# The partition sum of each conditioning gate: four paced pieces of 512 columns in place of one of 2048

## The chip, the cores and the metric

The kernel runs on one core of one Trainium2 chip. The metric is the device time of one execution in microseconds (us); less is better. The engines are TensorE (PE, its weight loads PEld), VectorE (DVE), ScalarE (ACT), GpSimd (POOL) and SyncE (SP), which run side by side and wait for each other by semaphores.

## The reference

A two-layer diffusion backbone over 256 latent and 256 context positions of width 2048. Layer 0 mixes by neighbourhood attention, layer 1 by a gated MLP (gMLP); a SwiGLU feed-forward network (FFN) follows each.

```
sh1, sc1, g1, sh2, sc2, g2 = split(silu(c) @ ada_w[i] + ada_b[i], 6)   # per layer i
y = mixer_i(h * (1 + sc1) + sh1)
h = layer_norm(ALPHA * h + g1 * y)
h = layer_norm(ALPHA * h + g2 * swiglu(h * (1 + sc2) + sh2))
...
# gMLP mixer: u, v = split(gelu(a @ w_in));  v = layer_norm(v)
#             return (u * (W_s @ v + b_s)) @ w_out          # W_s 128x128 per group
```

The change touches g1 and g2, two vectors of 2048 numbers in each layer, four "gates" in all. Each is a matrix-vector product with a matrix of 2048x2048.

## The kernel before

**Stages.** Attention comes first (up to about 590 us), then layer 0's FFN (up to some 1310), the gMLP (up to some 1690) and layer 1's FFN. In each, PE multiplies activations by a stream of weights, in pieces of 1024 columns (512 for a part of w_k). SP issues the weights' DMAs. ACT rounds each piece to a high part (L93, names beginning with h: hwq, hwf, hwgo), and DVE subtracts that from it to get the low part (L94, names beginning with l: lwk, lwq, lwf, lwgo). PE makes three matmuls for each tile: L88 high x high, L89 and L90 with one low part (which of the two is the low one depends on the stage). Activations are split by the same lines (kl, vl, tl, glgo, gld); ql is at L460.

**The conditioning work** is spread over this stream as tasks. A gate is made on DVE: the 2048 rows of its matrix come as 16 row blocks of 128 (k = 0 to 15), each in two halves of 1024 columns (ag, DMAs issued on ACT's queue at L77, four buffers, `ADA`). Each half is multiplied by a number per partition and added to `gate`, a tile of 128 partitions x 2048 columns (L176). `gate` begins at zero in all partitions but one, which holds the bias (L170, L171, on POOL). When all 32 halves are in, a sum over the 128 partitions is left; POOL makes it with one partition_all_reduce in place (L191). The result is read only in the residual at the stage's end (L569). The other four vectors of a layer are made by dot products on DVE (ad, L152).

**What sets the order.** Tasks stand in a list. `pace` divides their total weight by a number of ticks (126 for attention, 245, 62 and 170 for the stages after it); each `tick` adds that rate to a credit, and each task is put into the program when the credit holds its weight of 0.5. `need` empties the list as far as a stage requires. The DMAs of the first three tasks in the list (`FETCH`) are issued ahead. The compiler's scheduler then sets each engine's own order from the program's, by its model of what is ready; weight streams keep theirs.

Three places are spoken of in the prediction. In attention, per head, PE makes kps (keys, from ah, al and hwk, lwk), qps (queries), the scores s (from kh, kl, qh, ql), and transposes (pt, L519) of p, the softmax's numerator, which ACT makes (L509) from s and from its row maxima nm, which DVE makes (L502, L504). In the gMLP, for each block nb, PE makes sp (L858, from vv and ws), DVE makes u in place from sp and u (L859), and PE transposes u (uvt, L863) for the product with w_gout (pogo, from hwgo, lwgo, ghgo, glgo). Last, the FFN's first product pf takes hwf and lwf.

Of the kernel before, what the change touches and what calls it, by code (L numbers as in the profile page):

```python
# [23 lines left out]
NB = D // 512  # L24
# [27 lines left out]
def hybrid_kernel(ctx: ExitStack, tc: tile.TileContext, i, out):  # L52
# [20 lines left out]
    gate = {}  # L73
# [19 lines left out]
        S.copy(hi, src)  # L93
        V.tensor_tensor(lo, src, hi.bitcast(F32), ALU.subtract)  # L94

# [1 line left out]
    queue, ready = [], []  # L97
    pos = {"n": 0, "bufs": 3, "wide": None}

# [36 lines left out]
        del ready[:k]  # L136
        return got

# [1 line left out]
    loaded = {}  # L140

    def dot_task(layer, t, nt, half):
        key = (layer, t, nt, half)

        def fetch():
            src = i["ada_t"][dot_index(layer, t, nt)]
            loaded[key] = load(src[:, half * 1024 : (half + 1) * 1024], f"ad{layer}{t}{nt}{half}")

        def run():
            r = loaded.pop(key)  # L150
            o = (cols2 if half else cols)[:, layer, t, :]
            V.scalar_tensor_tensor(  # L152
                r, r, 1.0, c_bc[:, half * 1024 : (half + 1) * 1024], ALU.mult, ALU.mult,
                accum_out=o[:, nt : nt + 1],
            )
            if nt == KT - 1 and half:
                o = cols[:, layer, t, :]
                V.tensor_tensor(o, o, cols2[:, layer, t, :], ALU.add)
                V.tensor_tensor(o, o, badj[:, layer, t, :], ALU.add)
        return [(layer, t), 0.5, run, fetch]  # L160

    def gate_task(layer, t, kt, half):
        key = (layer, t, kt, half)
        sl = slice(half * 1024, (half + 1) * 1024)

        def fetch():
            if kt == 0 and half == 0:
                g = outer.tile([P, D], F32, tag="gate", name=f"gate{layer}{t}")
                gate[(layer, t)] = g
                nc.gpsimd.memset(g, 0.0)  # L170
                nc.gpsimd.dma_start(g[0:1, :], i["ada_b_row"][layer, t : t + 1, :])  # L171
            loaded[key] = load(i["ada_g"][gate_index(layer, t, kt)][:, sl], f"ag{layer}{t}{kt}{half}")

        def run():
            g = gate[(layer, t)][:, sl]
            V.scalar_tensor_tensor(g, loaded.pop(key), c_col[:, kt, 0:1], g, ALU.mult, ALU.add)  # L176
        return [(layer, t), 0.5, run, fetch]
# [7 lines left out]
        split_into(gh, gl, src)  # L185
        return gh, gl

    def sum_task(layer, t):
        def run():
            g = gate[(layer, t)]  # L190
            nc.gpsimd.partition_all_reduce(g, g, P, ReduceOp.add)  # L191
        return [(layer, t), 0.5, run, None]

    tasks, side = [], []
# [8 lines left out]
    def add_tasks(layer, *ts):  # L203
        for t in ts:
            if t in (G1, G2):
                tasks.extend(gate_task(layer, t, k, e) for k in range(KT) for e in range(2))
                tasks.append(sum_task(layer, t))
            else:
                tasks.extend(dot_task(layer, t, k, e) for k in range(KT) for e in range(2))

# [21 lines left out]
    def pace(units):  # L232
        state["rate"] = sum(t[1] for t in tasks) / units

# [1 line left out]
    for kt in range(KT):  # L236
        enqueue(i["w_kv0"][kt], f"kv{kt}", (W0,))
        for at, h, k0 in EARLY:
# [33 lines left out]
    enqueue_out(i["w_gout"], KT, "wgo")  # L272
    enqueue_ffn(1)

# [1 line left out]
    oT = outer.tile([P, NH, NT], F32, tag="xT", name="oT")  # L276
    with tc.tile_pool(name="attnX", bufs=1) as px, ExitStack() as late:
        ah = px.tile([P, KT, 512], F32R, tag="ah", name="ah")
# [153 lines left out]
        def t_tile(name):  # L432
            return mp.tile([P, 512], F32, tag="t", name=name, bufs=2)

        add_tasks(0, G1, SH2, SC2)
        add_tasks(1, SH1)
        pace(126)
        pend = []
# [363 lines left out]

            project_out(FT, lambda f: gT(f)[:, 0, :], key, name, finish, extra, last)

    # layer 0
    m = Modulated(0, 0, SH2, SC2, "f0")
    free = ExitStack()
    pw = free.enter_context(tc.tile_pool(name="pw", bufs=1))
# [3 lines left out]
    )  # L812
    affine_tasks(h_t, i["ln_row"][0], "a0")
    add_tasks(0, G2)
    add_tasks(1, SC1, SH2, SC2)
    pace(245)
# [7 lines left out]

    ffn(0, m, (0, G2), "d0", begin, free)

    # layer 1
    m = m2[0]
    affine_tasks(h_t, i["ln_row"][1], "a1")
    add_tasks(1, G1)  # L830
# [184 lines left out]
```

## Time and profile before

| | us |
|---|---|
| time, median of 3 runs | 2494.54 |
| lowest, highest | 2493.43, 2497.09 |
| profiled execution, span | 2495.6 |
| PE busy | 2422.3 |
| DVE busy | 1758.7 |
| ACT busy | 1097.2 |
| POOL busy | 110.6 |

The page of the profile gives for the profiled execution its span alone. Busy times of engines overlap, so they don't add up to the span. In the rows further below, the times in a row are the start (us from the span's begin) and how long it took; what stands in brackets is the engine's idle time just before and what ended it.

### The profile page before, as it was taken

Reading aid. Unit: us, or ns where it says so; the run is one execution under the profiler, and the core shown is the slowest. Engines: PE = TensorE matmul, PEld = TensorE weight load, DVE = VectorE, ACT = ScalarE, POOL = GpSimd, SP = SyncE. Lnnn points to the kernel's source line nnn. Section 1 sums busy time; section 2 is a strip of 40 time slices with the busy share of each in tenths; the row PEclk is TensorE's granted clock in tenths of the full one; section 3 lists DMA queues with packets and bytes.
Section 4 is the critical chain, followed back from the end, with each engine's and each line's share of the span. In section 5 each row is a group of like instructions: output and inputs, shape, how many; then the busy total and the mean of one; then the engine's idle time right before and its main releaser. Section 6 shows DMA issues by size and latency. Waiting matters only on the chain.

```text
span 2495.6 us, 38599 instructions
## 1 busy us (share of the span) xinstructions
PE 2422.3 (97%) x15254; PEld 2157.9 (86%) x15254; DVE 1758.7 (70%) x2159; ACT 1097.2 (44%) x1494; POOL 110.6 (4%) x56
## 2 busy tenths in 40 slices
PE   6999899999999999999999999899999999999998
PEld 5787788888789999999788778777899999998886
DVE  3878877777886676666778788687755555566666
ACT  3344433345553333333455554446533333344453
POOL 0000200000010020000000020020100000020000
PEclk8999999999999999999999999999999999999999
DMA  8977787777568878888888767765666666655563
GB/s 319 350 264 257 242 282 261 273 260 252 186 232 286 271 270 292 284 283 282 285 281 279 257 214 263 249 212 173 216 228 219 218 217 226 220 194 187 176 208 130
DMA packets 167422, 611.03 MB, mean 245 GB/s; under 512 B 18916, under 2 KB 21284, under 8 KB 162884
## 3 DMA queue, kind: packets, MB, share of 16 engines
q1 hardware_dynamic: 120888, 440.64, 52.8%
q10 hardware_dynamic: 46224, 167.89, 19.4%
q8 instruction: 119, 1.95, 0.3%
q14 instruction: 63, 0.52, 0.1%
q0 software_dynamic: 128, 0.03, 0.0%
HBM read 606.40 MB, written 2.10 MB: 244 GB/s over the span
## 4 chain that ended last, share of the span: by engine, by line
PE 85%; DVE 6%; DMA 5%; issue 1%; ACT 1%; POOL 0%; DVEq 0%; ACTq 0%
PE pf L90 12%; PE pf L88 12%; PE pf L89 12%; PE pod L90 6%; PE pod L89 6%; PE pod L88 6%; DMA ad<-in_ada_t 4%; PE vps L88 2%; PE vps L89 2%; PE vps L90 2%; PE gv L90 1%; PE gv L88 1%; PE gv L89 1%; PE powo L88 1%; PE kps L88 1%
## 5 line engine op out<-in xcount | busy, mean ns | idle before, releaser
L93 ACT CAST hwf<-rwf 128x1024 fp32r<-128x1024 f32 x320 | 335.8, 1049 | 556.9 <-PE pf L89 489.6
L94 DVE TENSOR_TENSOR lwf<-rwf,hwf 128x1024 fp32r<-128x1024 f32 x320 | 406.8, 1278 | 216.1 <-ACT hwf L93 215.3
L90 PE MATMUL pf<-f1h,lwf 128*128 128x256 f32 x1280 | 361.2, 282 | 0.3 <-DVE lwf L94 0.3
L90 PE MATMUL pf<-f0h,lwf 128*128 128x256 f32 x1280 | 361.1, 282 | 0.0
L88 PE MATMUL pf<-f1h,hwf 128*128 128x256 f32 x1280 | 361.0, 282 | 0.0
L88 PE MATMUL pf<-f0h,hwf 128*128 128x256 f32 x1280 | 361.0, 282 | 0.0
L89 PE MATMUL pf<-f0l,hwf 128*128 128x256 f32 x1280 | 360.7, 282 | 0.0
L89 PE MATMUL pf<-f1l,hwf 128*128 128x256 f32 x1280 | 360.6, 282 | 0.0
L152 DVE SCALAR_TENSOR_TENSOR ad<-ad,c_bc 128x1024 f32<-128x1024 f32 x192 | 233.9, 1222 | 167.6 <-DMA ad<-in_ada_t 167.3
L88 PE MATMUL pod<-hwd,ghd 128*128 128x512 f32 x684 | 267.9, 392 | 2.0 <-DVE gTb L796 2.0
L90 PE MATMUL pod<-hwd,gld 128*128 128x512 f32 x684 | 267.7, 392 | 0.4 <-DVE gld L94 0.4
L89 PE MATMUL pod<-lwd,ghd 128*128 128x512 f32 x684 | 267.8, 391 | 0.0
L94 DVE TENSOR_TENSOR lwd<-rwd,hwd 128x1024 fp32r<-128x1024 f32 x172 | 211.9, 1233 | 50.0 <-ACT hwd L93 49.2
L90 PEld LDWEIGHTS pf<-f1h,lwf 128*128 128x128 f32 x1280 | 242.5, 189 | 0.5 <-DVE lwf L94 0.5
L88 PEld LDWEIGHTS pf<-f1h,hwf 128*128 128x128 f32 x1280 | 242.6, 190 | 0.1
L89 PEld LDWEIGHTS pf<-f0l,hwf 128*128 128x128 f32 x1280 | 242.6, 190 | 0.0
L89 PEld LDWEIGHTS pf<-f1l,hwf 128*128 128x128 f32 x1280 | 242.6, 190 | 0.0
L88 PEld LDWEIGHTS pf<-f0h,hwf 128*128 128x128 f32 x1280 | 242.6, 190 | 0.0
L90 PEld LDWEIGHTS pf<-f0h,lwf 128*128 128x128 f32 x1280 | 242.6, 190 | 0.0
L176 DVE SCALAR_TENSOR_TENSOR gate<-ag,c_col,gate 128x1024 f32<-128x1024 f32 x128 | 165.1, 1296 | 87.0 <-DMA ag<-in_ada_g 86.5
L93 ACT CAST hwd<-rwd 128x1024 fp32r<-128x1024 f32 x172 | 180.0, 1046 | 43.3 <-DMA rwd<-in_w_out 19.1
L88 PEld LDWEIGHTS pod<-hwd,ghd 128*128 128x128 f32 x684 | 128.4, 188 | 30.8 <-DVE gTb L796 2.4
(331 smaller groups left out, 4568.1 us busy)
## 6 DMA issues: line engine op xcount, KB each, us to landing
rwf<-in_w_in_f SPq DMA_DIRECT2D x320, 512.0 KB
ad<-in_ada_t ACTq DMA_DIRECT2D x192, 512.0 KB
rwd<-in_w_out SPq DMA_DIRECT2D x176, 512.0 KB
ag<-in_ada_g ACTq DMA_DIRECT2D x128, 512.0 KB
rwg<-in_w_gin SPq DMA_DIRECT2D x64, 512.0 KB
ap<-in_ada_p SPq DMA_DIRECT2D x19, 1024.0 KB
rwq<-in_w_q SPq DMA_DIRECT2D x32, 512.0 KB
rwo<-in_w_o SPq DMA_DIRECT2D x32, 512.0 KB
```

The costliest lines, as they stand in the source:

```text
L88: keep(T.matmul(ps, sh, mh, start=first, stop=False))
L89: keep(T.matmul(ps, sh, ml, start=False, stop=False))
L90: keep(T.matmul(ps, sl, mh, start=False, stop=last))
L93: S.copy(hi, src)
L94: V.tensor_tensor(lo, src, hi.bitcast(F32), ALU.subtract)
L152: V.scalar_tensor_tensor(r, r, 1.0, c_bc[:, half * 1024 : (half + 1) * 1024], ALU.mult, ALU.mult, accum_out=o[:, nt : nt + 1],)
L176: V.scalar_tensor_tensor(g, loaded.pop(key), c_col[:, kt, 0:1], g, ALU.mult, ALU.add)
```

## The change

`sum_task` gets a number n and sums 512 columns of the gate; `add_tasks` puts four of them (NB is 4) behind the gate's 32 accumulations, each with a weight of 0.5 of its own. The other lines of the diff remove comments.

```
-    def sum_task(layer, t):
+    def sum_task(layer, t, n):
         def run():
-            g = gate[(layer, t)]
+            g = gate[(layer, t)][:, n * 512 : (n + 1) * 512]
             nc.gpsimd.partition_all_reduce(g, g, P, ReduceOp.add)
         return [(layer, t), 0.5, run, None]
...
                 tasks.extend(gate_task(layer, t, k, e) for k in range(KT) for e in range(2))
-                tasks.append(sum_task(layer, t))
+                tasks.extend(sum_task(layer, t, n) for n in range(NB))
```

The tasks of the attention stage weigh 66 in place of 64.5, those of the stage that ends with layer 0's FFN the same, those of the gMLP stage 18 in place of 16.5, and those of the last stage the same. As the program's order moves, so do the scheduled orders of the engines. Names carry a number at their end, which differs between the two programs.

DVE at the first gate, before (a gate row is the accumulation of one half):

```order
L94 TENSOR_TENSOR lwq_1024_2312<-rwq_1024_2309,hwq_1024_2311 128x1024
L286 TENSOR_TENSOR oT<-kps_2308,oT 128x512
L176 SCALAR_TENSOR_TENSOR gate_1471<-ag_2328,c_col,gate_1471 128x1024
L94 TENSOR_TENSOR kl_2335<-oT,kh_2334 128x512
L94 TENSOR_TENSOR lwk_0_2342<-rwk_0_2339,hwk_0_2341 128x512
L176 SCALAR_TENSOR_TENSOR gate_1471<-ag_2331,c_col,gate_1471 128x1024
L94 TENSOR_TENSOR lwq_0_2375<-rwq_0_2372,hwq_0_2374 128x1024
L460 SCALAR_TENSOR_TENSOR ql_2403<-qps_2338,qh_2402 128x256
L176 SCALAR_TENSOR_TENSOR gate_1471<-ag_2370,c_col,gate_1471 128x1024
L94 TENSOR_TENSOR lwq_1024_2411<-rwq_1024_2408,hwq_1024_2410 128x1024
L502 TENSOR_TENSOR s_2434<-s_2434,bias_2432 128x256
```

And after, at the same place:

```order
L176 SCALAR_TENSOR_TENSOR gate_1471<-ag_2331,c_col,gate_1471 128x1024
L94 TENSOR_TENSOR kl_2338<-oT,kh_2337 128x512
L94 TENSOR_TENSOR lwk_0_2345<-rwk_0_2342,hwk_0_2344 128x512
L94 TENSOR_TENSOR lwq_0_2376<-rwq_0_2373,hwq_0_2375 128x1024
L176 SCALAR_TENSOR_TENSOR gate_1471<-ag_2334,c_col,gate_1471 128x1024
L94 TENSOR_TENSOR lwq_1024_2412<-rwq_1024_2409,hwq_1024_2411 128x1024
L460 SCALAR_TENSOR_TENSOR ql_2404<-qps_2341,qh_2403 128x256
L94 TENSOR_TENSOR vl_2550<-v_2306,vh_2549 128x512
L286 TENSOR_TENSOR oT<-kps_2408,oT 128x512
L502 TENSOR_TENSOR s_2431<-s_2431,bias_2429 128x256
L502 TENSOR_TENSOR s_2443<-s_2443,bias_2429 128x256
L504 TENSOR_REDUCE nm_2436<-s_2431 128x1
```

The last accumulation of half 0 (of ag_2331 in both) moved from behind lwk to ahead of kl; that of half 1 (ag_2370 before, ag_2334 after) stays between the two lwq; ql moved behind both lwq, and vl and oT ahead of the scores.

DVE in the gMLP, at the u of the last two blocks, before:

```order
L94 TENSOR_TENSOR lwgo_1_1024_15343<-rwgo_1_1024_15340,hwgo_1_1024_15342 128x1024
L859 SCALAR_TENSOR_TENSOR u_15175<-sp_15362,bs,u_15175 128x2x128
L859 SCALAR_TENSOR_TENSOR u_15175<-sp_15373,bs,u_15175 128x2x128
L94 TENSOR_TENSOR lwgo_2_0_15396<-rwgo_2_0_15393,hwgo_2_0_15395 128x1024
L859 SCALAR_TENSOR_TENSOR u_15175<-sp_15362,bs,u_15175 128x2x128
L859 SCALAR_TENSOR_TENSOR u_15175<-sp_15373,bs,u_15175 128x2x128
L176 SCALAR_TENSOR_TENSOR gate_14025<-ag_15482,c_col,gate_14025 128x1024
L176 SCALAR_TENSOR_TENSOR gate_14025<-ag_15507,c_col,gate_14025 128x1024
L859 SCALAR_TENSOR_TENSOR u_15358<-sp_15416,bs,u_15358 128x2x128
```

And after:

```order
L94 TENSOR_TENSOR lwgo_1_1024_15355<-rwgo_1_1024_15352,hwgo_1_1024_15354 128x1024
L176 SCALAR_TENSOR_TENSOR gate_14031<-ag_15350,c_col,gate_14031 128x1024
L859 SCALAR_TENSOR_TENSOR u_15187<-sp_15377,bs,u_15187 128x2x128
L859 SCALAR_TENSOR_TENSOR u_15187<-sp_15388,bs,u_15187 128x2x128
L176 SCALAR_TENSOR_TENSOR gate_14031<-ag_15371,c_col,gate_14031 128x1024
L859 SCALAR_TENSOR_TENSOR u_15187<-sp_15377,bs,u_15187 128x2x128
L859 SCALAR_TENSOR_TENSOR u_15187<-sp_15388,bs,u_15187 128x2x128
L94 TENSOR_TENSOR lwgo_2_0_15411<-rwgo_2_0_15408,hwgo_2_0_15410 128x1024
L94 TENSOR_TENSOR glgo_4_15526<-uT,ghgo_4_15525 128x256
L859 SCALAR_TENSOR_TENSOR u_15373<-sp_15431,bs,u_15373 128x2x128
```

After, the two gate rows are the last of their halves (k = 15), and no accumulation of this gate follows; before, the two gate rows stand behind the four u, and one more accumulation, the last, follows behind the last u (not shown).

## Rows read from the trace of the kernel before

**Rows 1.** The page's busy times: engine, busy us, share of the span, instructions.

```profile
PE 2422.3 (97%) x15254; PEld 2157.9 (86%) x15254; DVE 1758.7 (70%) x2159; ACT 1097.2 (44%) x1494; POOL 110.6 (4%) x56
```

**Rows 2.** PE's waits over the whole span: what waited, its releaser, us in total, times, the longest.

```profile
PE pt L519 <- ACT p L509: 10.6, 6, 6.8
...
PE sp L858 <- DVE u L859: 5.7, 2, 4.9
...
PE kps L90 <- DVE lwk L94: 2.1, 3, 1.2
...
PE pogo L90 <- DVE glgo L94: 1.0, 1, 1.0
...
PE pf L90 <- DVE lwf L94: 0.3, 1, 0.3
```

**Rows 3.** POOL's timeline, the four sums.

```profile
267.92 12.78 POOL L191 PARTITION_ALL_REDUCE gate<-gate  x1 [110.16 <-DVE gate L176]
...
874.37 12.78 POOL L191 PARTITION_ALL_REDUCE gate<-gate  x1 [146.73 <-DVE gate L176]
...
1649.11 12.78 POOL L191 PARTITION_ALL_REDUCE gate<-gate  x1 [88.58 <-DVE gate L176]
...
2196.57 11.88 POOL L191 PARTITION_ALL_REDUCE gate<-gate  x1 [414.06 <-DVE gate L176]
```

**Rows 4.** DVE's timeline from 262 to 290 us, around the first sum.

```profile
261.46 1.28 DVE L176 SCALAR_TENSOR_TENSOR gate<-ag,c_col,gate 128x1024 f32<-128x1024 f32 x1 [1.32 <-DMA ag<-in_ada_g]
262.67 0.69 DVE L94 TENSOR_TENSOR kl<-oT,kh 128x512 fp32r<-128x512 f32 x1
263.27 0.68 DVE L94 TENSOR_TENSOR lwk<-rwk,hwk 128x512 fp32r<-128x512 f32 x1
...
265.06 1.22 DVE L94 TENSOR_TENSOR lwq<-rwq,hwq 128x1024 fp32r<-128x1024 f32 x1
...
270.73 0.68 DVE L286 TENSOR_TENSOR oT<-kps,oT 128x512 f32<-128x512 f32 x1
271.32 7.15 DVE L94 TENSOR_TENSOR lwk<-rwk,hwk 128x512 fp32r<-128x512 f32 x1
278.40 1.21 DVE L152 SCALAR_TENSOR_TENSOR ad<-ad,c_bc 128x1024 f32<-128x1024 f32 x1
```

**Rows 5.** PE's timeline in the same stretch, three of its matmuls.

```profile
264.27 0.39 PE L90 MATMUL kps<-ah,lwk 128*128 128x512 f32 x1
...
267.01 0.39 PE L90 MATMUL s<-kh,ql 128*128 128x512 f32 x1
...
280.50 0.48 PE L519 MATMUL pt<-ident,p 128*128 128x128 f32 x1 [6.80 <-ACT p L509]
```

**Rows 6.** DVE's timeline, the operation beside each of the three later sums.

```profile
875.33 10.15 DVE L94 TENSOR_TENSOR lwf<-rwf,hwf 128x1024 fp32r<-128x1024 f32 x1
...
1650.06 9.35 DVE L94 TENSOR_TENSOR glgo<-uT,ghgo 128x256 fp32r<-128x256 f32 x1
...
2197.00 9.78 DVE L94 TENSOR_TENSOR lwf<-rwf,hwf 128x1024 fp32r<-128x1024 f32 x1
```

**Rows 7.** The instructions of line 604 (counts; shortest, median and longest in ns; first and last start; form), which run beside POOL's broadcasts of 512 columns; POOL's last two broadcasts, of 2048 columns; and two DVE rows there, the first just ahead of the broadcasts and the second beside one.

```profile
L604 DVE TENSOR_TENSOR h_t<-h_t,lra x24: 677/683/1150, 708.1 to 1783.2; 128x512 f32<-128x512 f32 x24
...
2244.84 5.40 POOL L82 PARTITION_BROADCAST last_rows<-last_rows  x2 [36.39 <-DMA last_rows<-in_ln_row]
...
2244.13 0.43 DVE L94 TENSOR_TENSOR gld<-gTa,ghd 128x256 fp32r<-128x256 f32 x1
...
2248.00 2.38 DVE L94 TENSOR_TENSOR gld<-gTa,ghd 128x256 fp32r<-128x256 f32 x1
```

**Rows 8.** Windows: stretch, its length, then busy us of PE, PEld, DVE, ACT and POOL with instructions in brackets, PE's granted clock (1.00 is full), the DMA share and GB/s.

```profile
280.50:284.00 3.50, 3.50 (x13) 3.12 (x14) 3.50 (x7) 2.94 (x6) 0.20 (x1) 0.50 0.20 78
284.00:288.00 4.00, 4.00 (x22) 3.50 (x22) 3.06 (x4) 1.33 (x3) 0.00 (x0) 0.89 0.77 209
...
200.00:206.00 6.00, 3.91 (x25) 3.17 (x24) 5.56 (x8) 2.60 (x4) 0.00 (x0) 1.00 0.89 298
```

**Rows 9.** The gMLP from 1570 to 1585 us: two DMA issues on ACT's queue, and DVE up to the first u.

```profile
1571.02 0.33 ACTq L77 DMA_DIRECT2D ag<-in_ada_g  x1
...
1573.52 0.34 ACTq L77 DMA_DIRECT2D ag<-in_ada_g  x1
...
1578.12 1.28 DVE L176 SCALAR_TENSOR_TENSOR gate<-ag,c_col,gate 128x1024 f32<-128x1024 f32 x1 [3.13 <-DMA ag<-in_ada_g]
...
1580.46 0.87 DVE L859 SCALAR_TENSOR_TENSOR u<-sp,bs,u 128x256 f32<-128x256 f32 x2
```

**Rows 10.** The gMLP from 1632 to 1648 us: DVE at an accumulation, at the first two u after it, at the last u and at the last accumulation, and PE at the one wait there.

```profile
1632.16 1.28 DVE L176 SCALAR_TENSOR_TENSOR gate<-ag,c_col,gate 128x1024 f32<-128x1024 f32 x1 [2.09 <-DMA ag<-in_ada_g]
...
1634.49 0.87 DVE L859 SCALAR_TENSOR_TENSOR u<-sp,bs,u 128x256 f32<-128x256 f32 x2
...
1645.03 0.48 DVE L859 SCALAR_TENSOR_TENSOR u<-sp,bs,u 128x256 f32<-128x256 f32 x1
...
1647.72 1.28 DVE L176 SCALAR_TENSOR_TENSOR gate<-ag,c_col,gate 128x1024 f32<-128x1024 f32 x1
...
1635.03 0.48 PE L858 MATMUL sp<-vv,ws 128*128 128x256 f32 x1 [0.86 <-DVE u L859]
```

## The prediction

> **What bounds the kernel now.** I read the page's busy times first: PE is busy for 2422.3 us of a span of 2495.6, POOL, which makes the sums, for 4% [rows 1]. So the kernel is bound by TensorE, and an edit on POOL can only be worth PE's idle time, some 70 us in all, or cause more of it. Second, PE's waits by releaser [rows 2]: five lines can be tied to the places where a sum runs. Third, POOL's own timeline [rows 3]: the four sums take 12.78, 12.78, 12.78 and 11.88 us. Fourth, VectorE's rows just behind each sum's start, since nobody waits for a sum itself for hundreds of us, but VectorE stands still beside it. At the first sum, lwk<-rwk,hwk took 7.15 us where the same form took 0.68 eight us earlier [rows 4]. PE then waited 6.80 us for p at 280.50 [rows 5]. At the other three, lwf took 10.15 us, glgo 9.35 and lwf 9.78 [rows 6]; with a free port a 128x1024 subtraction takes 1.22 [rows 4] and a 128x256 one 0.43 [rows 7]. So a sum of 2048 columns holds a VectorE operation with two SBUF inputs for 10.15 - 1.22 = 8.93 us. An operation that reads PSUM is not held: oT<-kps,oT took 0.68 at 270.73, inside the sum that began at 267.92 [rows 3, 4].
>
> What the hold costs PE differs by place, by how far VectorE is ahead. First gate: 6.80 us [rows 5], and behind it a lower clock: 0.50 granted in 280.5 to 284 and 0.89 in 284 to 288 (0.50 is 1.2 GHz, 1.00 is 2.4), which loses 3.5 x 0.50 + 4 x 0.11 = 2.2 us [rows 8]. Second gate: no line of PE's waits stands there, so VectorE's lead was above 8.93. Third: 0.98 us (pogo<-glgo). Fourth: 0.3 us (pf<-lwf), a lead of about 8.56 - 0.3 = 8.3 [rows 2, 6]. All that the four sums cost is thus 6.8 + 2.2 + 1.0 + 0.3 = 10.3 us, and the change can't win more than that from them.
>
> **The change, part by part.** *Price of one piece.* No sum of 512 columns is in the trace. The bounds are 8.93 us (all of it fixed) and 8.93 / 4 = 2.23 (all of it columns). The nearest rows are POOL's broadcasts: the longest h_t subtraction beside a 512-column broadcast took 1.150 against 0.683, 0.47 more [rows 7]; gld beside one of 2048 columns (two last_rows broadcasts, 5.40 us each by the record's pair) took 2.38 against 0.43, 1.95 more [rows 7]. That is 4.2 to 1, with no fixed part to be seen. I take 2.23.
>
> *Pieces 0 and 1 start earlier.* Columns 0 to 1023 are complete with the half-0 accumulation of k = 15; only half 1 follows. So two pieces may run before the last accumulation, two after.
>
> *First gate.* I step through VectorE's order of after with the durations of before. Half 0 ends at 262.75 (its wait was for its DMA, which the change hardly moves) [rows 4]. Piece 0 holds from about 263.35 (kl runs first) to 265.6; lwk (0.68) is done at 266.2, where PE's L90 of kps stood at 264.27: 1.9 lost [rows 5]. lwq runs (1.22); piece 1 holds 267.4 to 269.6 with the half-1 accumulation behind it, done 270.9; lwq, then ql at 272.4, which the order has moved behind them. PE's L90 of s, at 267.01 before [rows 5] and 1.9 later now, would need it by 269: 3.4 lost. Piece 2 holds vl from 272.0 to 274.2; oT, two s and two nm read PSUM or have one input and cover piece 3. They end near 277.5, then kl, sm and p near 279.0. PE's transposes stand 17 matmuls earlier in PE's order, so PE is there at 276.9: 2.1 lost. The sum is 7.4 against 6.8, so **+0.6 us**, from -4 (one exposed piece less) to +4. As one stall of 6.8 becomes three of 1.9 to 3.4, the clock could come back: stalls adding up to 2.1 us in 200 to 206 left it at 1.00 [rows 8]. I count nothing for it, and up to -2.2 in the range.
>
> *Just after it.* Two ad accumulations (1.21 each, [rows 4]) fall out of the row there, so VectorE is up to 2.4 us earlier in front of the 1.2 us wait of kps on lwk [rows 2]. I take half of that wait: **-0.6 us**.
>
> *Second and fourth gate.* The halves' accumulations lie apart by a few other operations. Two pieces hold at most 2 x 2.23 = 4.5 us at a time, under the lead of 8.3. So nothing at the second, and the fourth's 0.3 goes: **-0.3 us**. What is late next there is the ordinary weight stream, which is on time now.
>
> *Paces.* Each piece is a task of 0.5, so a gate adds 2.0 in place of 0.5. In the stages with 129 tasks that makes 132, 2% more per tick; in those with 33 it makes 36, 9% more. Each task's DMA on ACT's queue goes out earlier too, and so do its accumulations. Where PE waits for VectorE directly, in the gMLP stage, this matters twice.
>
> *gMLP, first four u.* In after's order one more accumulation stands in front of them. Its data are the DMA issued at 1573.52. The DMA issued at 1571.02 ended the wait of the accumulation at 1578.12, 7.1 us later [rows 9], so this one lands near 1580.6. The accumulation (1.28) then ends near 1581.9, where the first u began at 1580.46: 1.4 late, less what the freed lwg's place gives. **+1.2 us**, from 0 (the DMA goes out earlier than this) to +2.5. This adds to a PE stall that is there already, 4.9 us of sp on u [rows 2].
>
> *gMLP, the sum.* It moves from 1649 to about 1633.5, where half 0 of k = 15 now stands (the accumulation at 1632.16) [rows 10]. Half 1 now stands between the u operations, not behind them. The u of L859 read PSUM and aren't held themselves, but what precedes each on VectorE's queue is. Piece 0 holds to 1635.8, the half-1 accumulation runs to 1637.1, pieces 1 to 3 hold two-input operations until about 1646.9; the last u then ends near 1649.4 in place of 1645.03 [rows 10]. PE's transposes of u follow each within a microsecond, so this is +4.4; the 0.98 of pogo and the 0.87 of sp at 1635.03 [rows 2, 10] go: **+2.5 us**, from -1.9 (the holds fall on work that nobody waits for) to +6.
>
> Sum: 0.6 - 0.6 - 0.3 + 1.2 + 2.5 = +3.4, a span of 2499.0. The profiled execution is 1.06 above the median of the runs shown (2495.6 against 2494.54), so the forecast is 2499.0 - 1.06 = 2497.9 us.
>
> **What the notes on the chip say.** VectorE's hold ended some 2.9 us before the sum's own record: that ends at 267.92 + 12.78 = 280.70, and lwk at 278.47, let go some 0.65 earlier, near 277.8 [rows 3, 4]. The Trainium skill (SBUF — State Buffer, "Who interferes with whom") calls the shared port pair an exclusive lock, held for the whole instruction by whoever issues first; the trace agrees that PSUM readers pass, not that the lock lasts as long as the record. By whole records a piece would cost 12.78 / 4 = 3.2 us, which is the third rival's lower price.
>
> **Rivals.** *1, faster: the lead swallows all but one piece.* Between pieces VectorE catches up, and only one hold of 2.23 reaches PE at the first gate. Then -4.6 there, -2.2 of clock, -0.98 - 0.87 at the third, -0.3 at the fourth, and no delay of u: -8.9, 2485.6 us. For it: the PE waits are small when VectorE is ahead by several us [rows 2]. Against it: at the first gate PE reads lwk 0.3 us after it is made [rows 4, 5]. [...] *2, slower: in the gMLP stage the sums land on the u operations*, and nothing is saved there: 0.6 + 1.2 + 4.4 - 0.3, and a clock step like the one of rows 8 behind the longer stall, +2.2: +8.1, 2502.6 us. It decides by whether the half-1 accumulation and pieces 1 to 3 run before the last u at 1645.03; before, that accumulation came at 1647. For it: the order; against: POOL may start a piece late. *3, slower: a piece isn't a quarter.* At 3.2 us each, seven exposed holds (three at the first gate, four at the third) cost 1 us more: +3.4 + 7, 2505 us. At 8.93 each these seven cost 47 more and the second and fourth gates lose about 20 each, near 2585. Against it: the 4.2 to 1 of rows 7. *4, it doesn't do what it says: POOL keeps the port through a pair of pieces*, so that holds are 4.5 long. First gate: lwk done at 268.5 (4.2 lost), the second pair holds lwq and vl into 275.5, p near 281: about 10 lost, +3 on the forecast, 2501 us.
>
> **How the numbers follow.** A measurement of this kernel tells about 0.2% (5 us) from no change: 2489.5 to 2499.5. The forecast has 0.46; its own range is 2493 to 2499.5. Rival 1 has 0.20 (2483 to 2489.5), rival 2 0.20 (2500 to 2506), rival 3 0.08 (most of it near 2505, 0.02 far above), rival 4 0.06. So faster 0.20, same 0.46, slower 0.34. The range from 2487 to 2506 leaves out about half of rival 1, the far part of 3 and the edge of 2.
>
> **What would show it.** In the changed profile: four records on POOL for each gate, of about 3.2 us; the VectorE operations beside them 2.2 us over their usual length (8.9 would be rival 3, 4.5 rival 4). Between 264 and 282 PE waits for lwk, ql and p of 2 to 3.5 us each (one wait of 2 would be rival 1), with the granted clock behind them. Between 1576 and 1582 the first u about 1 us later against its sp; between 1633 and 1650 PE waits for u or uT, together 2 to 4 us, and no 0.98 at pogo. The prediction is wrong if the POOL pieces start much later than their accumulations, if VectorE's order on the chip lets ql run before piece 1, or if PE's own order moves waits elsewhere in the two attention stages' worth of ticks by more than 5 us.

## The result and the profile after

The changed kernel's median is 2500.53 us (22 runs, 2490.25 to 2507.91) against 2494.81 for the kernel before (22 runs, 2482.52 to 2502.16). The ratio is 1.0025 with a 95% interval of 1.0015 to 1.0035, so it is slower by some 6 us (4 to 9). Single runs of either kernel spread over 18 to 20 us, so the ratio says more than any one run. The profiled span is 2498.0 against 2495.6; the run with that span has a time of 2499.77, 1.8 more. So this pair of traces shows 2.4 us of the loss; what more the times tell has to come from the experiments.

**Where it went.** PE runs the same 15254 matmuls in both kernels. How much later the n-th of them starts in the changed kernel's trace than in that of the kernel before shows where time is lost, whatever the engines' waits are called (PE's order differs in some places of the attention stage; each row stands where both kernels are at the same operation):

```
matmul n, its start before (us), later by (us)
 1640     258   -1.0     ahead of the first gate's sum
 1900     308   -2.8     behind it
 3800     688   -2.2     end of the attention stage and its projection
 9200    1507   -3.1     ahead of the gMLP's first u
 9530    1591   -0.1     behind it
 9710    1632   -0.1     ahead of the last eight u
 9840    1662   +4.1     behind them
10300    1771   +2.9
15253    2483   +2.4
```

The first gate got 1.8 us cheaper, and the gMLP stage lost 7.2 (3.0 up to and at its first u, 4.2 at its last). A shift of -1.7 is there already at matmul 400 (63 us), ahead of the first conditioning task (its DMA is issued at 164); that much two executions differ by themselves. From there to the end the change loses 4.1 us in this pair.

**First gate, after.** DVE's timeline; the last bracket, where there is one, is the idle time before:

```profile
262.55 0.68 DVE L94 TENSOR_TENSOR kl<-oT,kh 128x512 fp32r<-128x512 f32 x1
263.15 2.73 DVE L94 TENSOR_TENSOR lwk<-rwk,hwk 128x512 fp32r<-128x512 f32 x1
265.81 1.21 DVE L94 TENSOR_TENSOR lwq<-rwq,hwq 128x1024 fp32r<-128x1024 f32 x1
266.94 3.26 DVE L176 SCALAR_TENSOR_TENSOR gate<-ag,c_col,gate 128x1024 f32<-128x1024 f32 x1
...
271.26 0.41 DVE L460 SCALAR_TENSOR_TENSOR ql<-qps,qh 128x256 fp32r<-128x256 f32 x1
271.59 2.39 DVE L94 TENSOR_TENSOR vl<-v,vh 128x512 fp32r<-128x512 f32 x1
```

The one operation of 7.15 us [rows 4] has become three that are 1.7 to 2.1 us over their free length (2.73 - 0.68, 3.26 - 1.28, 2.39 - 0.68), with free operations between them. PE's timeline shows who waits, in place of the one wait of 6.80 [rows 5]:

```profile
265.94 0.50 PE L90 MATMUL kps<-ah,lwk 128*128 128x512 f32 x1 [2.55 <-DVE lwk L94]
...
271.72 0.80 PE L90 MATMUL s<-kh,ql 128*128 128x512 f32 x1 [2.77 <-DVE ql L460]
...
278.08 0.33 PE L519 MATMUL pt<-ident,p 128*128 128x128 f32 x1
```

These are 5.3 us, and the third wait, for p, is gone. The clock still falls behind the second of them: in the windows below (columns as in [rows 8]) it is at 0.50, which is 1.2 GHz, from 271.7 to 275.0. That loses 3.3 x 0.50 = 1.7 us, where it was 2.2 before. From 280 on, where it was at 0.50 and 0.89 before, it is at full speed. In the gMLP it falls once more, where it was at 1.00 before: behind PE's wait of 2.22 us for u, which ended at 1643.56, it loses 3 x 0.37 + 3 x 0.20 = 1.7 us.

```profile
271.70:275.00 3.30, 3.28 (x11) 2.89 (x12) 3.30 (x4) 0.38 (x1) 3.30 (x2) 0.50 0.73 273
...
280.00:284.00 4.00, 4.00 (x30) 3.66 (x29) 3.08 (x5) 2.74 (x5) 0.00 (x0) 1.00 0.63 198
...
1640.00:1643.00 3.00, 1.34 (x6) 0.75 (x4) 3.00 (x2) 1.13 (x2) 3.00 (x2) 1.00 0.37 117
1643.00:1646.00 3.00, 2.44 (x7) 1.97 (x8) 2.11 (x4) 0.00 (x0) 3.00 (x2) 0.63 0.27 75
1646.00:1649.00 3.00, 3.00 (x13) 2.39 (x13) 0.60 (x2) 1.63 (x3) 1.72 (x1) 0.80 0.42 157
```

**POOL, after**: the pieces at the first gate and in the gMLP (x2, x4: as many pieces with no gap that is told).

```profile
262.74 7.37 POOL L191 PARTITION_ALL_REDUCE gate<-gate  x2 [106.73 <-DVE gate L176]
270.29 7.35 POOL L191 PARTITION_ALL_REDUCE gate<-gate  x2 [0.18 <-DVE gate L176]
...
1634.15 13.57 POOL L191 PARTITION_ALL_REDUCE gate<-gate  x4 [76.27 <-DVE gate L176]
```

The first piece started behind half 0, where the single sum had started at 267.92 and 1649.11 [rows 3]. Four pieces take 13.6 to 14.7 us of POOL in place of 12.8.

**The gMLP, after**: DVE at the first u, and then from the last accumulation to the last u.

```profile
1576.77 1.28 DVE L176 SCALAR_TENSOR_TENSOR gate<-ag,c_col,gate 128x1024 f32<-128x1024 f32 x1 [4.82 <-DMA ag<-in_ada_g]
...
1579.15 1.28 DVE L176 SCALAR_TENSOR_TENSOR gate<-ag,c_col,gate 128x1024 f32<-128x1024 f32 x1
1580.35 0.87 DVE L859 SCALAR_TENSOR_TENSOR u<-sp,bs,u 128x256 f32<-128x256 f32 x2
...
1636.05 1.42 DVE L176 SCALAR_TENSOR_TENSOR gate<-ag,c_col,gate 128x1024 f32<-128x1024 f32 x1 [1.22 <-DMA ag<-in_ada_g]
...
1638.18 2.51 DVE L94 TENSOR_TENSOR lwgo<-rwgo,hwgo 128x1024 fp32r<-128x1024 f32 x1
1640.61 2.49 DVE L94 TENSOR_TENSOR glgo<-uT,ghgo 128x256 fp32r<-128x256 f32 x1
1643.03 0.47 DVE L859 SCALAR_TENSOR_TENSOR u<-sp,bs,u 128x256 f32<-128x256 f32 x1
...
1650.49 0.48 DVE L859 SCALAR_TENSOR_TENSOR u<-sp,bs,u 128x256 f32<-128x256 f32 x1
```

The last accumulation now runs at 1636, ahead of six u, where it ran at 1647.72 behind all of them [rows 10]; lwgo and glgo are held for 1.3 and 2.1 us between u and u, and the last u starts 5.5 us later, at 1650.49. Around them PE waits for u three times, and only the first of these waits has a like before (0.86 at 1635.03 [rows 10]):

```profile
1634.50 0.48 PE L858 MATMUL sp<-vv,ws 128*128 128x256 f32 x1 [1.15 <-DVE u L859]
...
1637.92 0.33 PE L863 MATMUL uvt<-ident,u 128*128 128x128 f32 x1 [0.92 <-DVE u L859]
...
1643.56 0.63 PE L858 MATMUL sp<-vv,ws 128*128 128x256 f32 x1 [2.22 <-DVE u L859]
```

PE's waits over the span (what waited, releaser, us, times, the longest), to be held against [rows 2]:

```profile
PE sp L858 <- DVE u L859: 9.0, 3, 5.6
PE pt L519 <- ACT p L509: 7.0, 6, 2.1
PE kps L90 <- DVE lwk L94: 2.8, 2, 2.5
PE s L90 <- DVE ql L460: 2.8, 1, 2.8
...
PE uvt L863 <- DVE u L859: 0.9, 1, 0.9
```

Pogo's wait of 1.0 and pf's of 0.3 are gone. Waits for u grew from 5.7 to 9.9 us in all.

### The profile page after: what moved, and what is told of

The parts are those of the page before. It is cut to its first block, busy times and chain, and to the rows that moved or that the text cites. A ratio compares the mean times of both kernels' runs of the same rounds, so it can differ in the third digit from the quotient of the medians.

```text
span 2498.0 us, 38630 instructions
## 1 busy us (share of the span) xinstructions
PE 2423.7 (97%) x15254; PEld 2157.8 (86%) x15254; DVE 1749.7 (70%) x2159; ACT 1097.8 (44%) x1494; POOL 119.4 (5%) x68
## 5 line engine op out<-in xcount | busy, mean ns | idle before, releaser
L94 DVE TENSOR_TENSOR lwf<-rwf,hwf 128x1024 fp32r<-128x1024 f32 x320 | 401.3, 1258 | 211.8 <-ACT hwf L93 210.7
```

## The experiments

Eleven kernels, each timed against the kernel before on the same chip. Two things change at once in the changed kernel: the sum comes in pieces, and the larger weight of a gate's tasks moves the order of DVE. The first two take them apart.

| | pieces | order of DVE | median | before | ratio, 95% interval |
|---|---|---|---|---|---|
| the change | 4 | moved | 2500.53 | 2494.81 | 1.0025 (1.0015 to 1.0035) |
| e1 | 4 | as before | 2488.19 | 2493.23 | 0.9989 (0.9975 to 1.0002) |
| e2 | 1 | moved | 2506.12 | 2493.23 | 1.0058 (1.0038 to 1.0077) |
| e3 | 4, gMLP 1 | moved, gMLP as before | 2492.03 | 2493.23 | 1.0002 (0.9986 to 1.0018) |
| e4 | gMLP 4 | gMLP moved | 2498.18 | 2493.23 | 1.0026 (1.0011 to 1.0041) |
| e5 | none | moved | 2490.35 | 2491.34 | 0.9998 (0.9983 to 1.0013) |
| e6 | none | as before | 2484.52 | 2491.34 | 0.9975 (0.9958 to 0.9992) |
| e7 | 4, late | as before | 2491.27 | 2491.34 | 0.9990 (0.9975 to 1.0004) |
| e8 | 4, gMLP 1 | as before | 2490.43 | 2491.34 | 0.9994 (0.9981 to 1.0007) |
| e9 | 4, gMLP late | as before | 2486.39 | 2493.84 | 0.9968 (0.9953 to 0.9983) |
| e10 | none | gMLP moved | 2491.15 | 2493.84 | 0.9987 (0.9971 to 1.0002) |
| e11 | none | moved, gMLP as before | 2488.15 | 2493.84 | 0.9971 (0.9955 to 0.9987) |

The traces bear out the third column. Of DVE's 2159 instructions all but 6, in layer 0's FFN, stand in the order of the kernel before in e1, e7, e8 and e9, and all of them in e6; in e5 all stand in the order of the changed kernel, and in e2 all but some 30, which lie ahead of the gMLP. e4 and e10 have one and the same order.

**e1, the pieces without the pace.** Against the changed kernel:

```
-        return [(layer, t), 0.5, run, None]
+        return [(layer, t), 0.125, run, None]
```

> Four pieces, but each with a task weight of 0.125, so that a gate's sums weigh 0.5 as before and VectorE's order is that of the kernel before. Theory A (the order is to blame: the heavier weight pulls the gMLP gate's last accumulations ahead of the last u, the split by itself is a gain): about 3 us under the kernel before (2 to 3 us of PE's 6.8 us wait at the first gate, 2.2 of the clock behind it, less 1 to 2 us in the gMLP, where pieces 0 and 1 still fall among the u). Theory B (the pieces are to blame: four holds of VectorE hit more than one, wherever they lie): 3 to 6 us above the kernel before, as the changed kernel is.

Measured: 0.9989, a median 5.0 us lower; so theory B, by which the pieces do the harm, falls. That e1 is faster than the kernel before is not shown, as its interval reaches 1.0002. DVE at the first gate, where the hold now falls on an accumulation and on lwq (and a third on vl, 2.58 us):

```profile
262.87 2.93 DVE L176 SCALAR_TENSOR_TENSOR gate<-ag,c_col,gate 128x1024 f32<-128x1024 f32 x1
265.72 3.33 DVE L94 TENSOR_TENSOR lwq<-rwq,hwq 128x1024 fp32r<-128x1024 f32 x1
```

PE waits there for 0.5 and 2.3 us, not for 6.8, and behind that the clock is at 0.50 for 3.4 us (from 275.6): 2.8 + 1.7 = 4.5 us in place of 6.8 + 2.2 = 9.0. Among the u pieces 0 and 1 still cost: waits of 1.5 (uvt) and 0.4 (sp) that the kernel before doesn't have.

**e2, the pace without the pieces.** Against the kernel before:

```
-        return [(layer, t), 0.5, run, None]
+        return [(layer, t), 2.0, run, None]
```

> One sum of 2048 columns with a task weight of 2.0: VectorE's order is that of the changed kernel, the hold is whole. Theory A: about 10 us above the kernel before, more than the changed kernel: at the first gate the hold of 8.9 us falls on vl, which stands ahead of the scores in this order (3 us more than before), and in the gMLP a hold from about 1638 to 1647 falls ahead of the last four u (6 to 8 us). Theory B: within 2 us of the kernel before, since there is one hold for each gate as before.

Measured: 12.9 us above by the medians, 1.0058 by the ratio (six runs), as theory A has it. DVE's two operations that were held, and PE's two largest waits:

```profile
266.04 9.28 DVE L94 TENSOR_TENSOR vl<-v,vh 128x512 fp32r<-128x512 f32 x1
```

```profile
1638.09 9.60 DVE L94 TENSOR_TENSOR lwgo<-rwgo,hwgo 128x1024 fp32r<-128x1024 f32 x1
```

```profile
PE pt L519 <- ACT p L509: 16.4, 6, 8.3
PE sp L858 <- DVE u L859: 12.3, 3, 7.2
```

In this order a whole hold of 8.6 us falls on vl, ahead of the scores (PE waits 8.3 for p, where it was 6.8), and one of 8.4 on a lwgo among the u (7.2 for sp, where there was none). The moved order is the harm; the pieces make it smaller.

**e3 and e4, gate by gate.** The choice is made where the tasks are added (`sum_task` also gets its number of columns, not shown); e4 has the opposite condition, `==`.

```
-                tasks.extend(sum_task(layer, t, n) for n in range(NB))
+                if (layer, t) != (1, G1):
+                    tasks.extend(sum_task(layer, t, n) for n in range(NB))
+                else:
+                    tasks.append(sum_task(layer, t, 0, D))
```

> The changed kernel, but the gate of the gMLP stage is summed whole, with the weight of 0.5: VectorE's order there is that of the kernel before, the other three gates stay as changed. Theory A: the loss is in the gMLP, so about 6 us under the changed kernel and about 1 us under the kernel before (2493 to 2495 on its scale). Theory B: the four pieces of the first gate cost as well, 2 us above the kernel before or more.

> The kernel before, but the gate of the gMLP stage alone is made in four pieces of weight 0.5. Theory A: the whole loss of the changed kernel and not the gain at the first gate, so 6 to 7 us above the kernel before. Theory B: a quarter to a third of the loss, 1 to 2 us above.

Measured: e3 1.0002 and e4 1.0026. The gMLP gate alone makes the whole loss of the change. The other three gates together are worth nothing that the times can tell, though PE's waits at the first gate are those of the changed kernel (2.9 and 2.8 us, and the clock at 0.50 from 271.6 for 3.4 us). In e4's trace the changed kernel's loss stands as it did there: PE waits 0.92 (uvt) and 2.23 us (sp) for u, and the clock is at 0.50 for 3.4 us from 1642.9.

**e5 and e6, no sums at all.** In both, `run` does nothing, so the gates stay unsummed. e5 is the changed kernel so cut, e6 the kernel before.

> The changed kernel with its tasks and order, but the sums themselves are left out (the gates stay unsummed over partitions). Theory A (the order matters only by where it puts the holds): about 10 us under the kernel before, and within 2 us of the other kernel without sums, e6. Rival C (the earlier accumulations and their DMAs cost by themselves, by the u that wait behind them): 3 us or more above e6, so some 7 us under the kernel before.

> The kernel before with its order, the four sums left out (the gates stay unsummed). This is the floor for any way of placing the sums in this order: 9 to 11 us under the kernel before (6.8 of waiting and 2.2 of clock at the first gate, 1.0 at the third, 0.3 at the fourth).

Measured: e6 0.9975, 6.8 us under, so the four sums cost the kernel before some 7 us by the medians (2.0 to 10.5 by the interval), where 9 to 11 were expected. e5 came at 0.9998, 5.8 above e6 by the medians. The intervals meet (0.9983 to 1.0013, 0.9958 to 0.9992), but this speaks for rival C: the moved order costs something even where no hold exists. It is more than theory A allows for. Leaving the sums out takes 0.27% off the changed kernel (1.0025 to 0.9998) and 0.25% off the kernel before: by the times, four pieces at the new places cost as much as one sum at the old ones, and the loss of the change is what the order costs by itself (0.23%). Intervals as wide as these don't show that, but it isn't ruled out either.

**e10 and e11, where the order costs.** No sums; the empty task weighs 2.0 in place of 0.5, in e10 for the gMLP's gate alone, in e11 for the other three.

> No sums (the gates stay unsummed); the order of the kernel before, but in the gMLP stage that of the changed kernel (the empty task weighs 2.0 there). If rival C's cost by order alone (5.8 us between e5 and e6) is in the gMLP (the accumulation that waits for its DMA ahead of the first u, another ahead of the last): 2 to 4 us above e6, 0.1 to 0.16% by the ratio to the kernel before. If not: within 1 us of e6.

> No sums (the gates stay unsummed); the order of the changed kernel in the attention stage and both FFN stages, that of the kernel before in the gMLP. If the cost by order alone is in the attention stage (dot products that wait for their DMA ahead of the scores): 3 us or more above e6. If it was a chance of those runs: within 1.5 us of e6, and e10 too.

Measured: e11 0.9971, e10 0.9987, so the attention and FFN stages lose nothing that the times can tell by their new order, and the gMLP perhaps 0.12% (3 us; the intervals of e10 and e6 overlap). The two don't add up to the 0.23% of e5; where the rest lies stays open. For the gMLP's gate alone, e4 and e10 have the same order with and without sums and differ by 0.39%, the kernel before and e6 by 0.25%. So the loss of e4 (0.26%) is about half order (0.12) and half holds (0.14), with an uncertainty as large as either. The row to look at is PE's wait for the first u, of e10 and then of e6:

```profile
PE sp L858 <- DVE u L859: 5.3, 1, 5.3
```

```profile
PE sp L858 <- DVE u L859: 3.8, 1, 3.8
```

PE's wait ahead of the first u, in the traces with the gMLP's order of before (the kernel before, e1, e3, e6, e7, e8, e9, e11), was 4.9, 2.9, 1.8, 3.8, 3.2, 4.6, 4.4 and 4.5 us, 3.8 on average; with the moved order (the change, e2, e4, e5, e10) it was 5.6, 4.7, 5.2, 4.0 and 5.3, on average 5.0. The 1.2 between them is the size that was forecast for the accumulation in front of the u. But 1.8 to 4.9 with one and the same order shows how much one run's DMAs decide.

**e7 and e8, the holds in another place.** e7 is e1 with the order of the pieces reversed by halves and pinned (kept in program order by `pin`, not shown), e8 is e1 with the gMLP's gate whole.

```
-                tasks.extend(sum_task(layer, t, n) for n in range(NB))
+                tasks.extend(sum_task(layer, t, n) for n in (2, 3, 0, 1))
```

> As e1 (four pieces of weight 0.125, VectorE's order of the kernel before), but the pieces are made in the order 2, 3, 0, 1 and pinned, so that none runs before the last accumulation of its gate. In the gMLP the four then lie behind the last u. Theory A (a hold costs by the place it falls on): no hold among the u, pogo's wait of 0.98 gone, and at the first gate most of the four holds lie beside scores and maxima, which read PSUM, so 1 to 3 us of the 6.8 stay; 6 to 8 us under the kernel before, 1 to 3 under e1. Theory B (each piece costs): not under e1.

> As e1, but the gMLP's gate is summed whole, as before. Theory A: the first gate's gain of e1 without the holds among the u: 1 to 2 us under e1, 6 to 7 us under the kernel before. Theory B: within 1 us of e1.

Measured: e7 0.9990, e8 0.9994: both miss the expected 6 to 8 and 6 to 7 us and stand at 1 to 3 by the ratio. For e7 the trace shows why. DVE at the first gate, and PE behind it:

```profile
273.68 2.58 DVE L94 TENSOR_TENSOR vl<-v,vh 128x512 fp32r<-128x512 f32 x1
...
276.79 3.26 DVE L152 SCALAR_TENSOR_TENSOR ad<-ad,c_bc 128x1024 f32<-128x1024 f32 x1
...
279.98 3.28 DVE L152 SCALAR_TENSOR_TENSOR ad<-ad,c_bc 128x1024 f32<-128x1024 f32 x1
...
283.93 0.58 PE L88 MATMUL o<-th,vh 128*128 128x256 f32 x1 [5.37 <-DVE tl L94]
```

One piece was covered by scores and maxima, as meant; the other three held vl and two dot products that stand ahead of tl, and PE waited 5.4 us for tl, with the clock at 0.51 from 281 to 288. At the third gate all went as theory A had it: no wait at pogo. For e8 the first gate's waits (0.9 and 2.3 us) are as in e1, and the clock is at 0.50 for 3.4 us behind them. So the gain there is 9.0 - 3.2 - 1.7 = 4.1 us and not the 6 that was expected without a clock step; the interval allows 4.7. Why it isn't lower by that much stays open.

**e9, each gate where it hurts least.** e1 with e7's order of pieces for the gMLP's gate alone, and all pieces pinned.

```
+                tasks.extend(sum_task(layer, t, n) for n in
+                             ((2, 3, 0, 1) if (layer, t) == (1, G1) else range(NB)))
```

> As e1 (pieces of weight 0.125, VectorE's order of the kernel before), with e7's late order of pieces for the gMLP's gate alone and the natural order for the other three. Theory A: e1's first gate (2.8 us of PE waits in place of 6.8, and no half clock behind them) and e7's third gate (no wait at pogo, no hold among the u): 5 to 7 us under the kernel before, 2 to 4 under e1. If gains at the first gate are given back later in the attention stage (the dot products' DMAs), 2 to 4 us under the kernel before.

Measured: 0.9968 (0.9953 to 0.9983), 7.5 us under the kernel before by the medians: faster than both kernels. That it is faster than e1 (0.9975 to 1.0002) is not shown, as the intervals meet. The first gate is not as expected: PE waits 1.6 and 2.3 us, and the clock is at 0.50 for 3.4 us from 278.8, in e1 as in e9. That is 5.6 us in place of 9.0; with the 1.0 of pogo and the 0.3 of pf the trace accounts for 4.7 us, within the interval (4.2 to 11.7). Pinned, three of the fourth gate's pieces also run only at 2244, behind a broadcast; PE doesn't wait there. In the gMLP every second DVE operation is held, and none of them is waited for:

```profile
1647.64 2.45 DVE L94 TENSOR_TENSOR glgo<-uT,ghgo 128x256 fp32r<-128x256 f32 x1
1650.01 1.21 DVE L94 TENSOR_TENSOR lwgo<-rwgo,hwgo 128x1024 fp32r<-128x1024 f32 x1
1651.15 2.46 DVE L94 TENSOR_TENSOR glgo<-uT,ghgo 128x256 fp32r<-128x256 f32 x1
```

## Why the prediction came out as it did

The wide range (2487 to 2506) held the time, the likeliest case did not: 2500.53 is 2.6 us above its 2497.9 and 1 us past the end of its own range (2499.5). It lies in the stretch of rival 2 (2502.6), which had a chance of 0.20. The ratio's interval, 0.15 to 0.35%, still reaches under the 0.2% that I took as the bound of what can be told from no change. That the sum came so near is in part luck: in the traces the first gate is 1.8 us better than forecast and the gMLP 3.5 worse.

Two readings in the working were off. The profiled span is set beside a median of times, and a time is 1.8 above its span; the forecast is the median plus 3.4 either way. And 1645.03 is where the last u starts; it ends at 1645.51, so +4.4 should have been +3.9.

**Price of a piece: right.** 2.23 was taken. 1.7 to 2.1 us were measured, 2.46 - 0.41 = 2.05 in the cleanest rows; lwgo's 1.3 is the exception. No fixed part shows, so rival 3 is out. Between the pieces of a pair nothing holds DVE: in e9 a lwgo of 1.21 us runs unhindered between two held glgo, as lwq does at the first gate of the changed kernel, so rival 4 is out too. The Trainium skill (SBUF — State Buffer, "Who interferes with whom") states that a DVE instruction with two SBUF inputs contends with a GpSimd instruction that reads SBUF, and calls the port pair that they share an exclusive lock. The traces agree in that such an operation is held and one that reads PSUM or has one input is not (two s took 0.75 us at 274.51 and two nm 1.27 at 275.17, beside a piece, against 0.76 and 1.28 before). The hold is shorter than POOL's record, which is rough: 2.05 us beside records of 3.6 to 4.1 in e9.

**First gate: right in where PE waits first, wrong in its sum.** Forecast: 1.9 for lwk, 3.4 for ql, 2.1 for p; measured: 2.55, 2.77 and nothing. DVE was some 0.7 us sooner than stepped (ql done at 271.7, not 272.4), and PE came to its transposes as p was ready. The clock, for which I counted nothing, did not come back as the range allowed: it fell behind the second wait and cost 1.7 in place of 2.2. Waits and clock are thus 7.0 us in place of 9.0, where +0.6 was forecast; the table has -1.8. Just after it, the 1.2 us wait of kps on lwk, of which I had taken half, is gone, and one of 0.85 for p, at 292, has come. The gain can't be found in the times: e3, which has it without the gMLP's loss, is at 1.0002. PE's later waits for p in the attention stage differ by several us from run to run, and hide it or take it back; which of the two, these runs don't tell.

**Second and fourth gate: right.** Nothing at the second (-2.2 at matmul 5000 and at 6000), pf's 0.3 gone at the fourth.

**gMLP, first u: mechanism right, size open.** +1.2 forecast, 0.7 by the two traces' waits (5.6 against 4.9), 1.2 by the means above; e10 against e6 gives 3 us with overlapping intervals. The 3.0 in the table of matmuls holds another 0.5 of waiting and 1.6 of clock: behind a wait of 2.1 us for lwg, at 1561, PE ran eight matmuls of 0.6 us, where they took 0.39 behind the kernel before's wait of 1.7. The clock step is in this trace alone. But the wait is in four of the five traces with the gMLP's moved order (2.1, 0.8, 1.4 and 0.2) and in one of the eight with the order of before, so some of it may belong to the order; the prediction has no term for it.

**gMLP, the sum: the term that was too small.** +2.5 forecast, 4.2 measured. Waits of 1.15 (sp), 0.92 (uvt) and 2.22 us (sp) stand in place of 0.86 and 0.98, 2.45 more: the sum as I made it. But the clock came on top, at 0.63 and 0.80 in the windows from 1643 to 1649, where it was 1.00 before: 1.7 us, and 2.45 + 1.7 is the 4.2. The 0.92, the 2.22 and the clock step stand in e4's trace too and are missing in those of e5 and e10, which have the same order without sums: they are the holds' doing. The step was rival 2's; its other condition, that the half-1 accumulation and the pieces run before the last u, was met to the letter (1636.05 against 1650.49). I should have given this rival the larger chance, as the order that I showed already met its condition. What it had wrong is that nothing is saved: the first gate and pogo did get cheaper.

**Rival 1** was right that dividing helps and wrong about when. With the moved order, pieces are the better: 1.0025 (1.0015 to 1.0035) against e2's 1.0058 (1.0038 to 1.0077), each against its own runs of before. With the order kept, e1 points the same way (0.9989, not clear of 1). The Trainium skill (Perfetto Trace Analysis, "Optimizing Scalar/DVE Operations") says of ScalarE and VectorE that breaking up instructions may let work finish sooner where these engines aren't saturated but make others idle. Here the divided instructions are POOL's, and the change against e2 shows the like for them.

**What stays open.** The loss is in the gMLP (e3, e4), and it comes with the moved order (e1, e2). The traces give the holds between the u 4.8 us of it (0.92, 2.22 and 1.7), less the 1.0 of pogo; e5 suggests that the earlier accumulations cost as much by themselves. How the two make up the 6 us of the times, these runs don't tell.

## What to carry to other kernels

Where one task's length holds another engine, ask for each place how far the held engine is ahead of the one that waits for it; the same 2 us cost nothing in an FFN, and 1 to 3 us each where PE waits for VectorE directly. An edit that adds paced tasks changes the pace, and so the order of everything in the stage: give the pieces the weight of the whole (e1) before judging the division itself, and then try them behind the last operation that is waited for (e9). When single runs spread by 20 us and the effect is 6, line up the n-th instruction of the bound engine in two traces, and check by switching the places one by one.

## What was not expected

Four short holds in a row don't have to fall on four operations in a row. In e9 the gMLP's glgo were held four times over (2.45 us each) and each lwgo between them ran free (1.21): a piece takes 3.6 to 4.1 us of POOL there and holds for 2.05 of them. At the first gate in e7 it was two dot products in a row (3.26 and 3.28), with only the short read of a result between them.

The whole cost of the sums, by leaving them out, was 6.8 us (e6, 0.9975) by the medians, less than the 10.3 that the waits and the clock at the four places add up to; the interval (2.0 to 10.5 us) still holds that number. e9 (0.9968) is not measurably above that floor.
